# Attention units that take two key groups at once, with scores in both row halves and PSUM copies on ScalarE

## The chip, the cores and the metric

The kernel runs on one core of one Trainium2 chip. The metric is device microseconds for one execution, a median over several runs; a profiled execution gives the trace that is read here. The engines are named as in the profile: PE (TensorE matmul) and PEld (its weight loads), DVE (VectorE), ACT (ScalarE), POOL (GpSimd) and SP (SyncE, which issues most loads).

## What is computed

Two decoder layers over 256 tokens of width 2048, all in float32. Cut to what matters:

```python
for l in range(DEPTH):
    h = rms_norm(x, norm1_g[l])
    z = h @ w_in[l]                  # sgu u | sgu v | q (16 heads) | k (4) | v (4)
    out_a = chunked_sgu(gelu(z_sgu), ...)
    out_b = swa_sink_attention(q, k, v, ...)
    x = x + concat(rms_norm(out_a), rms_norm(out_b)) @ w_out[l]
    h2 = rms_norm(x, norm2_g[l])
    x = x + (silu(h2 @ w_gate[l]) * (h2 @ w_up[l])) @ w_down[l]
```

The attention is banded: queries in blocks of 128, window 128, so block 0 sees 128 keys and block 1 sees 256. Sixteen query heads share four key groups (head h uses group h // 4), head width 64. q and k are RMS-normed per head; the scores get a relative-position bias from a table of 32 buckets, a mask, and a sink logit in the softmax.

## The kernel before

**Projections.** Every big product is split for precision: `split2` (lines 91 to 102) makes of each loaded 128x1024 weight tile `raw` a rounded part `wh` on ACT (line 97) and the rest `wl` on DVE (line 98); `mm3` (136 to 138) adds three matmuls of 128x512. `unit` (140) is one weight tile: 12 such matmuls over two token blocks, then `tick()`. A column block of `w_in` (`in_block`) is eight units. The order of blocks is k and v (block 6), q heads 0 to 7 (4), q heads 8 to 15 (5), gate v (2, 3), gate u (0, 1). Then come `w_out` (64 units over both layers), and the feed-forward part with a seven-product scheme (`seven`) interleaved with ordinary units. In this last part `debt` decides which stream goes next, from the constants VEC, MM and LOAD and the calls of `vec` and `pe`.

**What sets the order of small work.** `later(delay, fn)` puts a function into the program when the count of units has grown by `delay`; the framework then orders the instructions of each engine by its own scheduler, so a piece may stand a little earlier or later than written. All waits come from the framework.

**PSUM.** Pool `pa` (tag acc, 5 banks) holds the accumulators of the projections, `pd` (dacc, 2 banks) and `pm` (sm, 1 bank) serve small results in attention: `small_ps` (131) takes pm, pd, pd in turn.

**Attention.** `kv_norm` and `q_norm` evacuate an accumulator on ACT, square it on DVE (217), reduce (219), take the power on POOL (184), scale on DVE, transpose on PE (201) and copy the transposed tile out of PSUM on DVE with the gain (300, 323). k is written twice, so that each of the four groups stands in both row halves (partitions 0 to 63 and 64 to 127) of `kT`. `attend(g, t, par)` (341) handles one group and one query block. For t=0 a unit has all four heads of the group, two in each row half. For t=1 it has two heads only, of one row half (`par` is (0,) or (1,)), over 256 keys; the scores of one row half share a PSUM bank `ps_s`. The rest of a unit: add bias (361), maximum (366), small rows (369, 371), one exponential per head on ACT (374), es and rden (378 to 381); three units later `turn` transposes the probabilities (388) and copies them out on DVE (389); five units later `weigh` multiplies with v (395) and scales (405). There are 12 such units per layer, one every 2.25 units of weights. `attend_end` squares and transposes the result.

**The bias** is made on the chip: `rel_table` (243) multiplies the table with one-hot rows (`ps_r`, 251), writes it to DRAM (255), spreads it there by a skewed read (259), and `load_bias` (336) reads a group at a time.

**The end.** The last product's columns are added to `xres` (700) and sent out (703), 128x512 at a time.

Of the kernel before, what the change touches and what calls it, by code (L numbers as in the profile page):

```python
# [19 lines left out]
DRAM = bass.MemoryType.DRAM  # L20
# [30 lines left out]
RL = 512  # L51
WARM = 12

# [12 lines left out]
def trunk(ctx, tc, x, xt, w_in, w_out, w_gate, w_up, w_down, sgu_w, sgu_g, consts,  # L66
          rel_bias, onehot, radd, out):
# [8 lines left out]
    dp = ctx.enter_context(tc.tile_pool(name="dp", bufs=1, space=DRAM))  # L76
# [133 lines left out]
    def finish_rms(ss, width):  # L210
        tot = small([P, 1], "tot")
        nc.vector.tensor_reduce(tot, ss, AX.X, ALU.add)
        return inv_rms(tot, 1, width)

    def head_inv(z, n):
        sq = zp.tile([P, NB], F32, tag="z", name="sq")
        nc.vector.tensor_tensor(sq[:, : n * HD], z, z, ALU.mult)
        ss = small([P, n], f"hs{n}")
        nc.vector.tensor_reduce(
            ss, sq[:, : n * HD].rearrange("p (h d) -> p h d", d=HD), AX.X, ALU.add  # L220
        )
        return inv_rms(ss, n, HD)
# [5 lines left out]
    rdram = dp.tile([NH, P, SEQ], F32, tag="rdram", name="rdram")  # L228
    pairs1 = []
    ss1 = [small([P, ND], "ss4") for t in range(NTOK)]  # L230
# [6 lines left out]
    def load_x(t, h, ss=ss1):  # L237
        c = slice(h * D // 2, (h + 1) * D // 2)
        nc.sync.dma_start(xres[:, t, c], x[t * P : (t + 1) * P, c])
        for n in range(2 * h, 2 * h + 2):  # L240
            sum_sq(ss[t][:, n : n + 1], xres[:, t, n * NB : (n + 1) * NB])

    def rel_table():
        relb = cp.tile([NBUCKET, NH], F32, tag="relb", name="relb")
        nc.gpsimd.dma_start(relb, rel_bias)
        oneh = zp.tile([NBUCKET, RL], F32, tag="z", name="oneh")
        nc.gpsimd.dma_start(oneh, onehot)
        rad = zp.tile([NH, RL], F32, tag="z", name="rad")
        nc.gpsimd.dma_start(rad, radd)
        ps_r = small_ps([NH, RL], "ps_r")  # L250
        nc.tensor.matmul(ps_r, relb, oneh, start=True, stop=True)
        rsb = zp.tile([NH, RL], F32, tag="z", name="rsb")
        nc.vector.tensor_tensor(rsb, ps_r, rad, ALU.add)
        rline = dp.tile([NH, RL], F32, tag="rline", name="rline")
        nc.sync.dma_start(rline, rsb)
        skew = bass.AP(
            tensor=rline.tensor, offset=rline.offset + P - 1, ap=[[RL, NH], [-1, P], [1, SEQ]]
        )
        nc.sync.dma_start(rdram, skew)
# [7 lines left out]
    later(11, rel_table)  # L267

    for lay in range(L):
# [5 lines left out]
        def begin(lay=lay, layer=layer, ss1=ss1):  # L275
            layer["rstd1"] = [finish_rms(ss1[t], D) for t in range(NTOK)]
# [5 lines left out]
        kT = ap.tile([P, NKV, SEQ], F32, tag="big", name="kT", bufs=8)  # L282

        def kv_norm(acc, lay=lay, layer=layer, zkv=zkv, kT=kT):
            kd = []
            zz = ap.tile([P, NTOK, NB], F32, tag="big", name="zkv", bufs=8)
            for t in range(NTOK):
                z = zz[:, t]
                nc.scalar.activation(z, acc[t], AF.Copy, scale=layer["rstd1"][t])
                zkv.append(z)  # L290
                inv = head_inv(z[:, : NKV * HD], NKV)
                k2 = zp.tile([P, NKV, 2, HD], F32, tag="z", name="k2")
                kin = z[:, : NKV * HD].rearrange("p (h d) -> p h d", d=HD)
                for r in range(2):
                    nc.vector.tensor_tensor(k2[:, :, r, :], kin, bc(inv, HD), ALU.mult)
                kd.append(k2.rearrange("p h r d -> p (h r d)"))

            def to_T(c):
                ps = transpose_pair([kd[t][:, 2 * c * P : (2 * c + 2) * P] for t in range(NTOK)])
                nc.vector.tensor_scalar(  # L300
                    kT[:, 2 * c : 2 * c + 2, :], ps, cst[:, lay, C_KG : C_KG + 1], None, ALU.mult
                )

            for c in range(2):
                later(5 + c, lambda c=c: to_T(c))
# [5 lines left out]
        def q_norm(b, acc, lay=lay, layer=layer, qT=qT):  # L311
            qn = []
            for t in range(NTOK):
                z = zp.tile([P, NB], F32, tag="z", name="zq")
                nc.scalar.activation(z, acc[t], AF.Copy, scale=layer["rstd1"][t])
                inv = head_inv(z, 8)
                z3 = z.rearrange("p (h d) -> p h d", d=HD)
                nc.vector.tensor_tensor(z3, z3, bc(inv, HD), ALU.mult)
                qn.append(z)

            def to_T(c):
                ps = transpose_pair([qn[t][:, 2 * c * P : (2 * c + 2) * P] for t in range(NTOK)])
                nc.vector.tensor_scalar(
                    qT[b][:, 2 * c : 2 * c + 2, :], ps, cst[:, lay, C_QG : C_QG + 1], None,
                    ALU.mult,
                )

            for c in range(2):
                later(5 + c, lambda c=c: to_T(c))

        ssb = [small([P, NKV], "ss4") for t in range(NTOK)]
# [4 lines left out]
        def load_bias(g, bias=bias):  # L336
            bt = ap.tile([P, GRP, SEQ], F32, tag="big", name="bias", bufs=8)
            nc.gpsimd.dma_start(bt, rdram[g * GRP : (g + 1) * GRP].rearrange("h q k -> q h k"))
            bias[g] = bt

        def attend(g, t, par, zkv=zkv, kT=kT, qT=qT, ob=ob, bias=bias, layer=layer):
            nk = (t + 1) * P
            k0 = SEQ - nk
            nh = 2 * len(par)
            heads = [h for h in range(GRP) if h % 2 in par]
            step = heads[1] - heads[0]
            nkb = nk // P
            nsink = layer["nsink"]
            s = ap.tile([P, nh, nk], F32, tag="spt", name="s", bufs=4)
            for r in par:  # L350
                ps = small_ps([P, 2, nk], "ps_s")
                for i in range(2):
                    h = g * GRP + 2 * i + r
                    nc.tensor.matmul(
                        ps[:, i, :],
                        qT[h // 8][HD * r : HD * r + HD, (h % 8) // 2, t * P : (t + 1) * P],
                        kT[HD * r : HD * r + HD, g, :nk],
                        start=True,
                        stop=True,
                    )  # L360
                nc.vector.scalar_tensor_tensor(
                    s[:, par.index(r) :: len(par), :], ps, 1.0 / math.sqrt(HD),
                    bias[g][:, r::2, k0:], ALU.mult, ALU.add,
                )
            m = small([P, GRP], "m")[:, :nh]
            nc.vector.tensor_reduce(m, s, AX.X, ALU.max)
            hs = slice(g * GRP + heads[0], (g + 1) * GRP, step)
            nm = small([P, GRP], "nm")[:, :nh]
            nc.vector.scalar_tensor_tensor(nm, m, -1.0, nsink[:, hs], ALU.mult, ALU.min)
            es = small([P, GRP], "es")[:, :nh]  # L370
            nc.vector.tensor_tensor(es, nm, nsink[:, hs], ALU.subtract)
            den = small([P, GRP], "den")[:, :nh]
            for i in range(nh):
                nc.scalar.activation(
                    s[:, i, :], s[:, i, :], AF.Exp, bias=nm[:, i : i + 1],
                    accum_out=den[:, i : i + 1],
                )
            nc.scalar.activation(es, es, AF.Exp)
            rden = small([P, GRP], "rden")[:, :nh]
            nc.vector.tensor_tensor(rden, den, es, ALU.add)  # L380
            nc.vector.reciprocal(rden, rden)
            pt = ap.tile([P, nh * nkb, P], F32, tag="spt", name="pt", bufs=4)

            def turn():
                pst = small_ps([P, nh * nkb, P], "ps_p")
                s4 = s.rearrange("p h (b k) -> p (h b) k", k=P)
                for i in range(nh * nkb):
                    nc.tensor.transpose(pst[:, i, :], s4[:, i, :], ident)
                nc.vector.tensor_copy(pt, pst)

            def weigh():
                pv = small_ps([P, nh, HD], "ps_v")
                for i in range(nh):
                    for b in range(nkb):
                        nc.tensor.matmul(
                            pv[:, i, :],
                            pt[:, i * nkb + b, :],
                            zkv[b][:, (NKV + g) * HD : (NKV + g + 1) * HD],
                            start=b == 0,
                            stop=b == nkb - 1,  # L400
                        )
                if (g, t) not in ob:
                    ob[g, t] = zp.tile([P, GRP * HD], F32, tag="z", name="ob")
                o3 = ob[g, t].rearrange("p (h d) -> p h d", d=HD)
                nc.vector.tensor_tensor(o3[:, heads[0] :: step, :], pv, bc(rden, HD), ALU.mult)

            later(3, turn)
            later(5, weigh)

        def attend_end(g, lay=lay, ob=ob, ssb=ssb, pairs_b=pairs_b):  # L410
            for t in range(NTOK):
                sum_sq(ssb[t][:, g : g + 1], ob[g, t])
# [398 lines left out]
```

## Time and profile before

| | us |
|---|---|
| median of 3 runs | 1977.56 (1976.96 to 1980.13) |
| the profiled execution (its span) | 1981.0 |
| PE busy | 1956.6 |
| DVE busy | 1723.4 |
| ACT busy | 1151.8 |
| POOL busy | 127.0 |

The profiled execution is 3.4 us longer than the median of the runs. Weight tiles go through the chip in the order described: layer 1's `w_in` stage from 7 to 204 us, `w_out` to 295, feed-forward to 992, then the same again for layer 2, whose `w_in` stage ends at 1188 and `w_out` at 1279. The granted clock of PE is full throughout. In timeline rows the columns are start, duration (both us), engine, line, operation, tiles, shapes and count; what stands in brackets is idle time of the engine before the row and what ended it. [...]

### The profile page before, as it was taken

Reading aid. Unit: us, or ns where it says so; the run is one execution under the profiler, and the core shown is the slowest. Engines: PE = TensorE matmul, PEld = TensorE weight load, DVE = VectorE, ACT = ScalarE, POOL = GpSimd, SP = SyncE. Lnnn points to the kernel's source line nnn. Section 1 sums busy time; section 2 is a strip of 40 time slices with the busy share of each in tenths; the row PEclk is TensorE's granted clock in tenths of the full one; section 3 lists DMA queues with packets and bytes.
Section 4 is the critical chain, followed back from the end, with each engine's and each line's share of the span. In section 5 each row is a group of like instructions: output and inputs, shape, how many; then the busy total and the mean of one; then the engine's idle time right before and its main releaser. Section 6 shows DMA issues by size and latency. Waiting matters only on the chain.

```text
span 1981.0 us, 25159 instructions
## 1 busy us (share of the span) xinstructions
PE 1956.6 (99%) x8894; PEld 1592.8 (80%) x8894; DVE 1723.4 (87%) x1977; ACT 1151.8 (58%) x1463; POOL 127.0 (6%) x137
## 2 busy tenths in 40 slices
PE   9999999999999999999999999999999999999999
PEld 6788888778887888888888788877788878788887
DVE  6777689999999999999767766899999999999996
ACT  6465566665565565665654655665656555656553
POOL 1211001000000000000002100000000000000000
PEclk9999999999999999999999999999999999999999
DMA  8753657668777768768656445586687776687684
GB/s 316 255 167 129 190 167 225 218 209 247 223 231 235 223 213 259 220 220 265 202 190 190 141 152 178 177 253 195 214 251 218 231 246 202 207 272 209 221 268 141
DMA packets 119712, 424.46 MB, mean 214 GB/s; under 512 B 13169, under 2 KB 15345, under 8 KB 119585
## 3 DMA queue, kind: packets, MB, share of 16 engines
q1 hardware_dynamic: 107072, 377.65, 55.0%
q0 software_dynamic: 12512, 45.19, 12.9%
q8 instruction: 70, 1.15, 0.3%
q14 instruction: 58, 0.47, 0.1%
HBM read 420.66 MB, written 4.23 MB: 214 GB/s over the span
## 4 chain that ended last, share of the span: by engine, by line
PE 82%; DVE 8%; DMA 4%; issue 3%; ACT 2%; POOL 1%; ACTq 0%; SPq 0%; DVEq 0%; POOLq 0%
PE acc L136 9%; PE acc L138 9%; PE acc L137 9%; PE dacc L136 8%; PE dacc L137 8%; PE dacc L138 8%; PE m L137 6%; PE m L138 6%; PE m L136 6%; DVE wl L98 4%; PE n L137 3%; PE n L136 3%; PE n L138 3%; DMA raw<-in_w_down_dram 3%; ACT wh L97 2%
## 5 line engine op out<-in xcount | busy, mean ns | idle before, releaser
L97 ACT CAST wh<-raw 128x1024 fp32r<-128x1024 f32 (+1 forms) x778 | 801.0, 1049 | 652.7 <-DVE raw L609 232.8
L98 DVE TENSOR_TENSOR wl<-raw,wh 128x1024 fp32r<-128x1024 f32 (+1 forms) x778 | 927.4, 1217 | 130.1 <-PE acc L137 54.9
L136 PE MATMUL dacc<-wh,aT 128*128 128x512 f32 x608 | 237.1, 392 | 0.6 <-ACT wh L97 0.2
L137 PE MATMUL dacc<-wl,aT 128*128 128x512 f32 x608 | 237.2, 390 | 0.0
L138 PE MATMUL dacc<-wh,aT 128*128 128x512 f32 x608 | 236.8, 390 | 0.0
L137 PE MATMUL m<-wl,ext 128*128 128x512 f32 x576 | 227.6, 395 | 5.1 <-DVE wl L98 5.1
L136 PE MATMUL m<-wh,ext 128*128 128x512 f32 x576 | 226.9, 394 | 4.7 <-ACT wh L97 4.7
L138 PE MATMUL m<-wh,ext 128*128 128x512 f32 x576 | 224.5, 390 | 0.0
L98 DVE TENSOR_TENSOR wl<-t,wh 128x1024 fp32r<-128x1024 f32 x144 | 175.5, 1219 | 16.8 <-issue 8.0
L136 PE MATMUL acc<-wh,hT 128*128 128x512 f32 x448 | 180.3, 404 | 0.7 <-ACT wh L97 0.7
L97 ACT CAST wh<-t 128x1024 fp32r<-128x1024 f32 x144 | 151.4, 1051 | 47.9 <-PE dacc L138 30.7
L137 PE MATMUL acc<-wl,hT 128*128 128x512 f32 x448 | 175.6, 392 | 0.6 <-DVE wl L98 0.6
L138 PE MATMUL acc<-wh,hT 128*128 128x512 f32 x448 | 175.5, 392 | 0.0
L617 POOL DMA_DIRECT2D t<-in_w_gate_dram x72 | 61.4, 852 | 1374.5 <-DVE wl L98 721.0
L136 PE MATMUL acc<-wh,aT 128*128 128x512 f32 x352 | 139.2, 395 | 0.0
L138 PE MATMUL acc<-wh,aT 128*128 128x512 f32 x352 | 137.4, 390 | 0.0
L137 PE MATMUL acc<-wl,aT 128*128 128x512 f32 x352 | 137.2, 390 | 0.0
L136 PEld LDWEIGHTS dacc<-wh,aT 128*128 128x128 f32 x608 | 114.1, 188 | 26.4 <-DVE xres L700 2.3
L137 PEld LDWEIGHTS m<-wl,ext 128*128 128x128 f32 x576 | 108.1, 188 | 32.9 <-DVE wl L98 11.6
L137 PEld LDWEIGHTS dacc<-wl,aT 128*128 128x128 f32 x608 | 114.2, 188 | 24.7 <-DVE wl L98 1.5
L138 PEld LDWEIGHTS dacc<-wh,aT 128*128 128x128 f32 x608 | 114.1, 188 | 23.6
L136 PEld LDWEIGHTS m<-wh,ext 128*128 128x128 f32 x576 | 108.2, 188 | 30.1 <-ACT wh L97 8.0
(150 smaller groups left out, 3040.7 us busy)
## 6 DMA issues: line engine op xcount, KB each, us to landing
raw<-in_w_gate_dram SPq DMA_DIRECT2D x176, 512.0 KB, 5.6
raw<-in_w_up_dram SPq DMA_DIRECT2D x176, 512.0 KB, 4.5
raw<-in_w_down_dram SPq DMA_DIRECT2D x176, 512.0 KB, 5.3
raw<-in_w_in_dram SPq DMA_DIRECT2D x108, 512.0 KB, 4.3
t<-in_w_gate_dram POOLq DMA_DIRECT2D x72, 512.0 KB, 6.4
raw<-in_w_out_dram SPq DMA_DIRECT2D x64, 512.0 KB, 3.7
bias<-rdram POOLq DMA_DIRECT2D x8, 512.0 KB, 4.4
xr<-in_xt_dram SPq DMA_DIRECT2D x8, 256.0 KB, 5.7
```

Of the source, the lines that this page charges most:

```text
L97: nc.scalar.copy(wh[:, j : j + step, :], src)
L98: nc.vector.tensor_tensor(wl[:, j : j + step, :], src, f(wh[:, j : j + step, :]), ALU.subtract)
L136: nc.tensor.matmul(acc, ah, wh, start=first, stop=False)
L137: nc.tensor.matmul(acc, ah, wl, start=False, stop=False)
L138: nc.tensor.matmul(acc, al, wh, start=False, stop=last)
L617: nc.gpsimd.dma_start(t2, w_gate[lay, b, i, 1], accum_op=ALU.add)
```

## The change

- The host lays out the q columns of `w_in` so that the first q block holds groups 0 and 1, the second 2 and 3, and head i of group 2gp stands in row half 0 beside head i of group 2gp+1 in row half 1. k is then written once: `kT` holds two groups per transposed tile, in the two row halves.
- `attend(gp, t, i0, n)` takes two groups. t=0: four heads of each group, eight in all; t=1: two heads of each. There are 6 units per layer, at the counts in `UNIT_AT`. Scores alternate between the two row halves and go to two banks.
- `turn` comes two units after (before: three), in two banks of four transposes, and `weigh` four after (before: five).
- Copies out of PSUM of k, q and the probabilities go to ACT, as do the squares in `head_inv`; reductions and powers of the two token blocks share tiles.
- `small_ps` has a fourth bank in its turn, from `pa`.
- The bias comes from the host as `band`, one contiguous load per group; `rel_table` goes. The scratch for DMA descriptors is halved.
- The last column block is added and sent out in halves.

```diff
-        pool, tag = ((pm, "sm"), (pd, "dacc"), (pd, "dacc"))[next(turns) % 3]
+        pool, tag = ((pm, "sm"), (pd, "dacc"), (pd, "dacc"), (pa, "acc"))[next(turns) % 4]
...
+UNIT_AT = (6, 9, 12, 15, 19, 23)
...
+            nc.scalar.activation(sq[:, : n * HD], z, AF.Square)
...
-    later(11, rel_table)
...
-                for r in range(2):
-                    nc.vector.tensor_tensor(k2[:, :, r, :], kin, bc(inv, HD), ALU.mult)
+                nc.vector.tensor_tensor(k, kin, bc(inv[t], HD), ALU.mult)
...
+                ps = transpose_pair(kd)
+                nc.scalar.activation(kT, ps, AF.Copy, scale=cst[:, lay, C_KG : C_KG + 1])
...
-                nc.vector.tensor_scalar(
-                    qT[b][:, 2 * c : 2 * c + 2, :], ps, cst[:, lay, C_QG : C_QG + 1], None,
-                    ALU.mult,
+                nc.scalar.activation(
+                    qT[b][:, 2 * c : 2 * c + 2, :], ps, AF.Copy,
+                    scale=cst[:, lay, C_QG : C_QG + 1],
                 )
...
+            nc.gpsimd.dma_start(bt, band[g])
...
+            s = ap.tile([P, 2, n, nk], F32, tag="spt", name="s", bufs=4)
+            ps = [small_ps([P, n, nk], f"ps_s{r}") for r in range(2)]
+            for i in range(n):
+                for r in range(2):
+                    rows = slice(HD * r, HD * r + HD)
                     nc.tensor.matmul(
+                        ps[r][:, i, :], qT[gp][rows, i0 + i, t * P : (t + 1) * P], kT[rows, gp, :nk],
+                        start=True, stop=True,
                     )
+            for r in range(2):
                 nc.vector.scalar_tensor_tensor(
+                    s[:, r], ps[r], 1.0 / math.sqrt(HD), bias[2 * gp + r][:, isl, SEQ - nk :],
+                    ALU.mult, ALU.add,
                 )
...
             def turn():
+                for half in range(2):
+                    pst = small_ps([P, 4, P], "ps_p")
+                    for i in range(4):
+                        nc.tensor.transpose(pst[:, i, :], s8[:, 4 * half + i, :], ident)
+                    nc.scalar.copy(pt[:, 4 * half : 4 * half + 4], pst)
...
-            later(3, turn)
-            later(5, weigh)
+            later(2, turn)
+            later(4, weigh)
...
+        units = [(gp, t, i0, n) for gp in range(2) for t, i0, n in ((0, 0, GRP), (1, 0, 2), (1, 2, 2))]
...
+                    parts = 2 if final and lay == L - 1 and n == ND - 1 else 1
...
-    nc = bacc.Bacc("TRN2", target_bir_lowering=False, num_devices=1)
+    nc = bacc.Bacc("TRN2", target_bir_lowering=False, num_devices=1, dynamic_dma_scratch_size=8192)
```

Where the instructions stand now. The first place is on PE, in layer 1, at scores of t=1. `acc` is the running projection, `ps_s` scores, `ps_v` the product with v, `ps_p` transposed probabilities, `ps_t` other transposes. Before, one row half at a time:

```order
L138 MATMUL acc_810<-wh,hT 128x512
L354 MATMUL ps_s<-kT,qT_129 128x256 x2
L395 MATMUL ps_v<-zkv,pt 128x64 x4
L388 MATMUL ps_p<-ident,s 128x128 x4
L136 MATMUL acc_809<-wh,hT 128x512
```

and in the change (its lines are those of the new program, where 330 is the scores, 134 to 136 are `mm3`):

```order
L136 MATMUL acc_765<-wh,hT 128x512
L330 MATMUL ps_s_887<-kT,qT_125 128x256
L330 MATMUL ps_s_888<-kT,qT_125 128x256
L330 MATMUL ps_s_887<-kT,qT_125 128x256
L330 MATMUL ps_s_888<-kT,qT_125 128x256
L199 MATMUL ps_t<-ident,zq 128x128 x4
L134 MATMUL acc_764<-wh,hT 128x512
```

Two matmuls of one row half have become four that alternate between the halves and their banks; a layer has four such pieces where it had eight. Only the last unit of layer 2 is torn: its first bank is filled here, in the change, and its second 34 projection matmuls later:

```order
L415 MATMUL ps_g<-v,wm 128x128 x4
L330 MATMUL ps_s_9435<-kT,qT_8293 128x256 x2
L135 MATMUL acc_9215<-wl,hT 128x512
L136 MATMUL acc_9215<-wh,hT 128x512
L135 MATMUL acc_9216<-wl,hT 128x512
```

The piece stays two of one half, as before. The second place is PE at scores of t=0 before, with tile numbers (924 is the bank of row half 0, 928 that of row half 1):

```order
L138 MATMUL acc1_810<-wh_907,hT_188 128x512
L354 MATMUL ps_s_924<-kT_128,qT0_129 128x128 x2
L354 MATMUL ps_s_928<-kT_128,qT0_129 128x128 x2
L136 MATMUL acc0_809<-wh_950,hT_214 128x512
L137 MATMUL acc0_809<-wl_951,hT_214 128x512
```

These four, two of one half and then two of the other, become eight that alternate. The third place is ACT in the first softmax of layer 1. Before:

```order
L97 COPY wh<-raw 128x1024 x8
L374 ACTIVATE s,den<-s,nm 128x128 x4
L378 ACTIVATE es<-es 128x4
L97 COPY wh<-raw 128x1024
L315 ACTIVATE zq<-acc_573,ir_460 128x512
```

and in the change:

```order
L302 ACTIVATE qT_125<-ps_t,cst 128x512
L95 COPY wh<-raw 128x1024
L349 ACTIVATE s,den<-s,nm 128x128 x8
L353 ACTIVATE es<-es 128x8
L293 ACTIVATE zq<-acc_538,ir_441 128x512
L364 COPY pt<-ps_p 128x512 x2
L293 ACTIVATE zq<-acc_539,ir_441 128x512
L218 ACTIVATE sq<-zq 128x512 x2
```

Eight exponentials, both copies of the probabilities and two squares now stand between one `wh` cast and the next. From the first matmul of the seven-product scheme to the next layer's first k transpose, and again in layer 2 from its last `ob` transpose to the end, PE's rows are the same in both programs.

More of the change, by code (lines that the diff above doesn't have):

```diff
@@ L19 @@
 PSUM = bass.MemoryType.PSUM
-DRAM = bass.MemoryType.DRAM
 P = 128
@@ L227, in trunk @@
     xres = cp.tile([P, NTOK, D], F32, tag="xres", name="xres")
-    rdram = dp.tile([NH, P, SEQ], F32, tag="rdram", name="rdram")
     pairs1 = []
-    ss1 = [small([P, ND], "ss4") for t in range(NTOK)]
+    ss1 = small([P, NTOK, ND], "ss4")
     def first_pair(p, pairs=pairs1):
@@ L240, in load_x @@
         for n in range(2 * h, 2 * h + 2):
[L241 to L259, printed above, removed]
+            sum_sq(ss[:, t, n : n + 1], xres[:, t, n * NB : (n + 1) * NB])
     for p in range(2):
@@ L275, in begin @@
         def begin(lay=lay, layer=layer, ss1=ss1):
-            layer["rstd1"] = [finish_rms(ss1[t], D) for t in range(NTOK)]
+            layer["rstd1"] = finish_rms(ss1, D)
             nsink = small([P, NH], "nsink")
@@ L337, in load_bias, with attend @@
             bt = ap.tile([P, GRP, SEQ], F32, tag="big", name="bias", bufs=8)
-            nc.gpsimd.dma_start(bt, rdram[g * GRP : (g + 1) * GRP].rearrange("h q k -> q h k"))
+            nc.gpsimd.dma_start(bt, band[g])
             bias[g] = bt
-        def attend(g, t, par, zkv=zkv, kT=kT, qT=qT, ob=ob, bias=bias, layer=layer):
+        def attend(gp, t, i0, n, zkv=zkv, kT=kT, qT=qT, ob=ob, bias=bias, layer=layer):
             nk = (t + 1) * P
[L343 to L359, printed above, removed]
@@ L366, in attend @@
+            m, nm, es, den, rden = (row(v) for v in ("m", "nm", "es", "den", "rden"))
             nc.vector.tensor_reduce(m, s, AX.X, ALU.max)
[L367 to L372, printed above, removed]
@@ L391, in weigh @@
-            def weigh():
[L392 to L405, printed above, removed]
@@ new lines, in weigh @@
+            def weigh():
+                pv = small_ps([P, 2, n, HD], "ps_v")
+                for r in range(2):
+                    cols = slice((NKV + 2 * gp + r) * HD, (NKV + 2 * gp + r + 1) * HD)
+                    for i in range(n):
+                        for b in range(t + 1):
+                            nc.tensor.matmul(
+                                pv[:, r, i], pt[:, (r * n + i) * (t + 1) + b, :], zkv[b][:, cols],
+                                start=b == 0, stop=b == t,
+                            )
+                if (gp, t) not in ob:
+                    ob[gp, t] = zp.tile([P, NB], F32, tag="z", name="ob")
+                o4 = ob[gp, t].rearrange("p (r i d) -> p r i d", r=2, d=HD)[:, :, isl]
+                nc.vector.tensor_tensor(
+                    o4, pv, rden.unsqueeze(3).to_broadcast([P, 2, n, HD]), ALU.mult
+                )
@@ L452, in v_gate @@
                 later(6 + half, lambda half=half: spatial(half))
-        ssa = [small([P, 2], "ss2") for t in range(NTOK)]
+        ssa = small([P, NTOK, 2], "ssa")
         pairs_a = []
```

176 lines of the change are left out of this document (91 added, 85 removed).

## The prediction

> **What bounds the kernel now.** I read the page first, then busy time by stage, then PE's own waits.
>
> ```profile
> span 1981.0 us, 25159 instructions
> PE 1956.6 (99%) x8894; PEld 1592.8 (80%) x8894; DVE 1723.4 (87%) x1977; ACT 1151.8 (58%) x1463; POOL 127.0 (6%) x137
> PE 82%; DVE 8%; DMA 4%; issue 3%; ACT 2%; POOL 1%; ACTq 0%; SPq 0%; DVEq 0%; POOLq 0%
> ```
>
> PE is busy 99% of the span, and 82% of the chain that ended last is PE. The stages say the same where the change lies:
>
> ```profile
> 60.00:200.00 140.00, 138.57 (x720) 111.79 (x719) 105.89 (x200) 77.53 (x161) 19.04 (x18) 1.00 0.54 177
> 320.00:985.00 665.00, 658.16 (x2920) 537.97 (x2919) 625.80 (x606) 397.81 (x424) 28.93 (x34) 1.00 0.74 230
> 1050.00:1180.00 130.00, 128.54 (x677) 104.27 (x676) 98.24 (x191) 71.67 (x154) 18.98 (x16) 1.00 0.51 160
> 1300.00:1976.00 676.00, 668.28 (x2954) 544.70 (x2953) 628.79 (x609) 394.12 (x414) 29.67 (x35) 1.00 0.72 225
> ```
>
> The columns are the stretch, its length, busy time of PE, PEld, DVE, ACT and POOL, clock, DMA share and GB/s. In the two attention stretches (rows one and three) PE is idle 1.43 and 1.46 us, while DVE is busy 76% and ACT 55%. So time goes there only if PE's own stream gets shorter; DVE work that is removed or moved to ACT buys nothing by itself. In the feed-forward stretches DVE is at 94% and PE idles 6.8 and 7.7 us, but there the change alters no instruction of PE and its order is the same, so I leave them as they are. Most of PE's idle time in attention is three waits of the probability transposes, here by stretch:
>
> ```profile
> PE ps_p L388 <- DVE s L361: 0.6, 1, 0.6
> PE ps_p L388 <- DVE nm L369: 0.9, 1, 0.9
> PE ps_p L388 <- DVE s L361: 0.5, 1, 0.5
> ```
>
> **The change part by part.** What a small piece costs PE is the distance between the projection matmuls around it, less what these take themselves. First the scores of t=1:
>
> ```profile
> 79.52 0.39 PE L137 MATMUL acc<-wl,hT 128*128 128x512 f32 x1
> 79.75 0.39 PE L138 MATMUL acc<-wh,hT 128*128 128x512 f32 x1
> 80.07 1.13 PE L354 MATMUL ps_s<-kT,qT 64*128 64x256 f32 x4
> 81.13 0.50 PE L136 MATMUL acc<-wh,hT 128*128 128x512 f32 x1
> 81.46 0.40 PE L137 MATMUL acc<-wl,hT 128*128 128x512 f32 x1
> ```
>
> Projection matmuls start 0.23 us apart. From 79.75 to 81.46 there are 1.71 us with two of them, so the piece costs 1.71 - 0.45 = 1.26 us for two matmuls of one row half (each is two records). Whether the other half can run beside it is shown by t=0, whose four matmuls are two of one half and then two of the other:
>
> ```profile
> 95.01 0.39 PE L138 MATMUL acc<-wh,hT 128*128 128x512 f32 x1
> 95.33 0.72 PE L354 MATMUL ps_s<-kT,qT 64*128 64x128 f32 x8
> 95.98 0.50 PE L136 MATMUL acc<-wh,hT 128*128 128x512 f32 x1
> 96.32 0.39 PE L137 MATMUL acc<-wl,hT 128*128 128x512 f32 x1
> 95.33 0.39 PE L354 MATMUL ps_s<-kT,qT 64*128 64x128 f32 x2
> 80.39 0.38 PE L354 MATMUL ps_s<-kT,qT 64*128 64x256 f32 x1
> 80.60 0.59 PE L354 MATMUL ps_s<-kT,qT 64*128 64x256 f32 x2
> ```
>
> The last three rows are what was under way in windows of 50 ns. At 95.33 two records run at once, and both are over after 0.39 us, about as long as one takes; in the t=1 piece the window shows one alone from 80.39, and the next starts 0.21 later. So the halves run side by side. A piece of four alternating matmuls over 256 keys should cost what two of one half cost, 1.26, plus a few hundredths: I take 1.27. Bounds: 1.26 below, and above 1.26 + 4 x 0.21 = 2.10 if 256 columns did not overlap. I take the low end, since the row of t=0 is the same kind of matmul. Before there are 8 such pieces per layer, 16 x 1.26 = 20.2 us. After there are 8 in all, but the last of layer 2 is torn into two of one half: 7 x 1.27 + 2 x 1.26 = 11.4. **Saved 8.8.**
>
> Scores of t=0: from 95.01 to 96.32 are 1.31, less 0.45, so 0.86 for a piece of four. The step within one half at 128 columns is half of 0.21; four more records in each half make 0.86 + 4 x 0.11 = 1.30 for eight (at most 0.86 + 0.65, were the whole block repeated). After: 4 x 1.30 = 5.2. Before: 7 x 0.86 = 6.0, and the first piece of layer 1, which stands in three parts among other work:
>
> ```profile
> 62.38 1.04 PE L201 MATMUL ps_t<-ident,zq 128*128 128x128 f32 x8
> 64.05 0.48 PE L354 MATMUL ps_s<-kT,qT 64*128 64x128 f32 x2 [0.63 <-DVE qT L323]
> 66.18 0.40 PE L138 MATMUL acc<-wh,hT 128*128 128x512 f32 x1
> 73.67 0.39 PE L138 MATMUL acc<-wh,hT 128*128 128x512 f32 x1
> 74.74 0.39 PE L137 MATMUL acc<-wl,hT 128*128 128x512 f32 x1
> ```
>
> From 62.38 to 66.18 are 3.80; less eight transposes at 0.11 and three projection matmuls that is 2.24. The third part takes 74.74 - 73.67 - 0.45 = 0.62. Together 2.9, with the wait of 0.63 for the copy of q in it. In the new order this piece stands whole, with 12 projection matmuls (2.7 us) between the last q transposes and it, against the 0.6 us of a copy on ACT (row below). **Saved 6.0 + 2.9 - 5.2 = 3.7.**
>
> Transposes and the table:
>
> ```profile
> 83.75 0.39 PE L138 MATMUL acc<-wh,hT 128*128 128x512 f32 x1
> 83.98 0.60 PE L388 MATMUL ps_p<-ident,s 128*128 128x128 f32 x4
> 84.65 0.40 PE L137 MATMUL acc<-wl,hT 128*128 128x512 f32 x1
> 38.28 0.39 PE L138 MATMUL acc<-wh,hT 128*128 128x512 f32 x1
> 38.60 1.03 PE L251 MATMUL ps_r<-oneh,relb 32*16 32x512 f32 x2
> 39.90 0.40 PE L137 MATMUL acc<-wl,hT 128*128 128x512 f32 x1
> ```
>
> Four transposes cost 0.90 - 0.45 = 0.45; k needs four fewer per layer, **0.9**. The table matmul costs 1.62 - 0.45 = 1.17, **1.2**. The probability transposes (48 per layer) and the products with v keep their number, and since four full-height ones cost hardly more than their own steps, larger or smaller pieces of them gain nothing.
>
> The three waits of the turn (2.0 us in the rows above) depend on how far ahead of the turn the scores stand, against the softmax chain:
>
> ```profile
> 76.44 0.40 ACT L374 ACTIVATE s<-s,nm 128x128 f32<-128x128 f32 x1 [1.29 <-DVE nm L369]
> 76.84 0.39 ACT L374 ACTIVATE s<-s,nm 128x128 f32<-128x128 f32 x1
> 77.29 1.23 DVE L98 TENSOR_TENSOR wl<-raw,wh 128x1024 fp32r<-128x1024 f32 x1 [0.69 <-PE acc L137]
> 81.23 0.69 DVE L361 SCALAR_TENSOR_TENSOR s<-ps_s,bias 128x512 f32<-128x512 f32 x1
> 82.44 0.68 DVE L366 TENSOR_REDUCE m<-s 128x2 f32<-128x512 f32 x1
> L626 ACT COPY m<-m 128x512 f32<-128x512 f32 x18 | 10.4, 576 | 1.5 <-PE m L138 1.4
> L446 ACT ACT_TABLE_LOAD x4 | 5.1, 1283 | 3.8 <-PE acc L138 3.8
> ```
>
> A unit of t=0 now needs two bias adds (1.4), a maximum over twice the row (about 1.3), 0.2 for the small row and eight exponentials 0.40 apart (3.2): 6.1 us to the last, 4.5 to the fourth. In the first unit 24 projection matmuls stand between, 5.5 us, and the second bank's transposes come 0.45 later, at 6.0. It just fits; in units where the product with v stands between as well there are some 7 us. I take 0.5 of waits for all turns: **saved 1.5**. Against that I set **0.5** for new waits in the projections. On ACT 27 operations of about 0.58 per layer come on (twelve probability copies, five gains of k and q, ten squares): 15 us, so from 77.5 of 140 to about 93 of 132. In the order above some 7 us of such work stand between two `wh` casts (eight exponentials, two evacuations, two copies, two squares), and the three weight tiles that PE can still draw on cover 3 x 12 x 0.23 = 8.3.
>
> The rest costs nothing, for these reasons. The copies of k and q on ACT are hidden by the 12 projection matmuls that follow their transposes (2.7 us); without that cover each would cost PE its 0.6, five per layer. The moved squares and the shared powers lie in a chain of four weight units (11 us) from the projection's end to its transposes, where before there were five; the scheduler now puts these one unit earlier, and a late one would show as a wait for `zq`, of the size of the 0.63 above. The bias loads stand on POOL, ahead of the power of the second q block; with `kT` out of their buffers, the four groups, `zkv` and both `qT` are seven of eight, so the second pair need not wait, and POOL's power is not held up; if it were, a power late by one unit costs 2.7 per layer. [...] At the end two adds of half the width take about a tenth longer than one, and the last store is half as large: a few tenths either way, taken as 0.
>
> Sum: 8.8 + 3.7 + 0.9 + 1.2 + 1.5 - 0.5 = 15.6 us. The profiled span goes from 1981.0 to 1965.4; the runs lie 3.4 below their profile (1977.56 against 1981.0), so 1962.0.
>
> **The rivals.** *The softmax chain takes PE's place (slower).* Units are twice as large and ACT holds exponentials, copies and gelu in one queue. Place: the turn. Behind one `wl` (1.23), two table loads (1.28 each, to gelu and back) and a gelu of about 0.6 a chain grows by 4.4 us. The t=0 units (6.1 + 4.4 against 6.0) would wait 4.5 each; of the t=1 units (chain 4.9, with exponentials of 0.5, an estimate between once and twice the 0.40; 7.4 of cover) half would wait 1.9: 4 x 4.5 + 4 x 1.9 = 25.6, so 10 us slower net, 1988. It makes the kernel slower from 1.3 us of wait per unit on. For it: the three waits above are of this kind. Against: the new order puts at least 5.5 us between. [...]
>
> *Smaller gain by new waits.* A fourth bank of small tiles comes from the projections' five; where two of them are held when a block starts, its first matmuls wait for one evacuation, 0.6. Seven blocks per layer make 14 x 0.6 = 8.4 at most: 1962 to 1970, 1967 if over half of them wait.
>
> *256 columns do not overlap.* Then 7 pieces cost 0.84 more: 5.9, 1967.9. That is the case in which the change does not do what it says; the t=0 row speaks against it.
>
> *Feed-forward waits shrink too.* Its 14.5 us of idle PE could fall if it starts with more weights ready: 5 us, 1957. Same order, so unlikely.
>
> **How the numbers follow.** A measurement of this kernel tells 0.2% (4 us) from no change. Chances: forecast 0.64 (its own range 1958 to 1966), smaller gain 0.14, no overlap 0.05, feed-forward too 0.06, nothing visible 0.04, slower 0.07. All but the last two are faster by more than 4 us: 0.89; same 0.04; slower 0.07. The range of 8 in 10 runs from 1956 (the feed-forward case) to 1970 (both smaller-gain cases): it leaves out the slow rival and the rare ends.
>
> **What would show it.** In the profile of the change: score pieces of t=1 with eight records in about 1.15 us, seven such in place of eight torn ones; a projection matmul 1.7 us after the one before the piece; attention stretches shorter by about 8.5 us in layer 1 and 6.5 in layer 2; ACT near 70% there; PE's waits for probabilities under 1 us; feed-forward stretches of the same length. Wrong would be: score records one after the other, or PE waiting more than 1 us per unit for exponentials, or for a bank.

## The result, and the profile after

The kernel after takes 1971.88 us (median of 6 runs, 1970.31 to 1973.83) against 1977.26 us for the kernel before (6 runs, 1975.64 to 1980.13): ratio 0.9968, 95% interval 0.9958 to 0.9978. It is faster, by 5.4 us; 15.6 were forecast, and 1971.88 lies above the range.

The page of the profiled execution after: span and instructions, PE's row, engines of the chain that ended last.

```profile
span 1968.8 us, 24956 instructions
PE 1942.7 (99%) x8884; PEld 1586.9 (81%) x8884; DVE 1678.4 (85%) x1812; ACT 1175.8 (60%) x1489; POOL 115.5 (6%) x116
PE 85%; DVE 6%; issue 3%; ACT 2%; DMA 2%; POOL 1%; SPq 0%; DVEq 0%; ACTq 0%; POOLq 0%
```

The two profiles differ by 12.2 us, the runs by 5.4. A run of the kernel after takes 1.7 us more than its own span (1970.47 with 1968.8). By that the profiled execution before took about 1982.7, 5 us above the runs that were shown with it; a profile is one execution, and "the runs lie 3.4 below their profile" was no property of the kernel.

Busy time by stage (length; PE, PEld, DVE, ACT, POOL; clock; DMA share and GB/s), cut at the first and last projection matmul of a layer's input block and at the ends of the feed-forward. Before, then after:

```profile
7.40:204.10 196.70, 194.92 (x962) 156.65 (x963) 142.89 (x256) 111.78 (x215) 27.91 (x26) 1.00 0.64 216
295.30:991.90 696.60, 689.76 (x3066) 563.66 (x3064) 655.00 (x648) 418.62 (x457) 32.56 (x38) 1.00 0.73 228
991.90:1188.10 196.20, 194.74 (x978) 158.22 (x977) 139.07 (x250) 104.44 (x197) 28.42 (x24) 1.00 0.53 168
1279.30:1976.20 696.90, 689.18 (x3048) 561.82 (x3047) 648.57 (x639) 407.76 (x434) 32.73 (x38) 1.00 0.72 224
```

```profile
7.40:199.20 191.80, 187.31 (x956) 153.36 (x957) 120.72 (x176) 123.36 (x228) 24.30 (x17) 1.00 0.59 210
290.30:987.10 696.80, 689.99 (x3064) 563.46 (x3063) 654.42 (x646) 418.31 (x457) 31.54 (x37) 1.00 0.71 228
987.10:1179.40 192.30, 190.25 (x975) 155.52 (x974) 117.48 (x171) 116.46 (x210) 24.24 (x17) 1.00 0.50 172
1270.50:1964.00 693.50, 687.35 (x3049) 562.13 (x3047) 648.07 (x637) 408.16 (x434) 31.53 (x37) 1.00 0.71 225
```

Attention is shorter by 4.9 and 3.9 us, not by 8.5 and 6.5. In layer 1 PE's busy time fell by 7.6 us, but its idle time rose from 1.8 to 4.5. In layer 2 the busy time fell by 4.5 only: there much of the waiting stands between single transposes, and busy time covers it. The matmuls do what was forecast, in PE's order of time (start, duration):

```profile
71.02 1.16 PE L330 MATMUL ps_s<-kT,qT 64*128 64x128 f32 x16
72.11 0.50 PE L134 MATMUL acc<-wh,hT 128*128 128x512 f32 x1
81.40 1.13 PE L330 MATMUL ps_s<-kT,qT 64*128 64x256 f32 x8
```

A t=1 piece of eight records takes 1.13 us, a t=0 piece of sixteen 1.16: the halves overlap. The rest of the gain went into PE's waits (total, times, longest), first layer and then second:

```profile
PE ps_p L363 <- ACT s L349: 2.3, 1, 2.3
PE ps_v L372 <- DVE aT L190: 0.9, 1, 0.9
...
PE ps_v L372 <- DVE aT L190: 0.9, 1, 0.9
PE ps_p L363 <- ACT s L349: 0.9, 1, 0.9
```

The first one is followed back through the engines' rows in order of time (idle time and its releaser in brackets):

```profile
82.53 3.91 POOL L182 TENSOR_TENSOR ir<-ms,mhalf 128x16 f32<-128x16 f32 x1 [21.39 <-DVE ms L180]
86.47 1.29 DVE L298 TENSOR_TENSOR zq<-zq,ir 128x512 f32<-128x512 f32 x2 [2.83 <-POOL ir L182]
87.68 1.28 DVE L335 SCALAR_TENSOR_TENSOR s<-ps_s,bias 128x512 f32<-128x512 f32 x2
90.01 1.21 DVE L344 TENSOR_REDUCE m<-s 128x4 f32<-128x1024 f32 x1
91.93 0.51 ACT L349 ACTIVATE s<-s,nm 128x256 f32<-128x256 f32 x1 [5.37 <-DVE nm L345]
92.58 0.44 PE L363 MATMUL ps_p<-ident,s 128*128 128x128 f32 x2 [2.33 <-ACT s L349]
```

The scores of the second unit are ready at 82.5. VectorE stands 2.83 us for the merged power of the second q block, and both bias adds are queued behind that multiplication. ScalarE, meant to be the risk, stands idle for 5.37 us. At 125 us the same happens with v, and a transposed pair is evacuated late, whose bank the product with v needs:

```profile
125.01 1.29 DVE L428 TENSOR_TENSOR v<-v,ir 128x512 f32<-128x512 f32 x2 [3.04 <-POOL ir L182]
129.41 0.86 DVE L190 SCALAR_TENSOR_TENSOR aT<-ps_t,cst,aT 128x256 fp32r<-128x256 f32 x2
130.02 1.97 PE L372 MATMUL ps_v<-zkv,pt 128*128 128x64 f32 x16 [0.86 <-DVE aT L190]
```

### The profile page after: what moved, and what is told of

Its sections match the earlier page's. It is cut to its first block, busy times and chain, and to the rows that moved or that the text cites. A ratio compares the mean times of both kernels' runs of the same rounds, so it can differ in the third digit from the quotient of the medians.

```text
span 1968.8 us, 24956 instructions
## 1 busy us (share of the span) xinstructions
PE 1942.7 (99%) x8884; PEld 1586.9 (81%) x8884; DVE 1678.4 (85%) x1812; ACT 1175.8 (60%) x1489; POOL 115.5 (6%) x116
## 3 DMA queue, kind: packets, MB, share of 16 engines
q8 instruction: 69, 1.13, 0.2%
## 4 chain that ended last, share of the span: by engine, by line
PE 85%; DVE 6%; issue 3%; ACT 2%; DMA 2%; POOL 1%; SPq 0%; DVEq 0%; ACTq 0%; POOLq 0%
PE dacc L134 9%; PE dacc L135 9%; PE dacc L136 9%; PE acc L135 8%; PE acc L136 8%; PE acc L134 8%; PE m L135 7%; PE m L136 7%; PE m L134 7%; PE n L135 3%; PE n L136 3%; PE n L134 3%; DVE wl L96 3%; ACT wh L95 1%; DVE raw L596 1%
```

## The experiments

Each ratio is to the kernel before on the same chip, which took 1981.8 to 1982.3 us on these chips (1977.3 in the runs above). The changed kernel itself ran on only one of these chips, so variants on the other are compared with it by ratio (0.9972).

**Both kernels again**, unedited (three profiles).

> The kernel before, unchanged, for a second profile. If the profiled execution of 1981.0 us was one of its slow ones (its runs have a median of 1977.26, and the kernel after lies 1.7 above its own span in every run), this profile's span should be near 1975.5 and the missing 5.5 us should stand in the feed-forward stretches (idle PE 6.8 and 7.7 us in the first profile), with both attention stretches the same to 0.3 us. If profiling itself adds 3.4 us to this kernel, as the prediction took it, the span is again 3 to 4 us above the median of its runs.

> The changed kernel, unchanged, for a second profile. If the waits in attention are fixed by the order, the wait of 2.3 us for the exponentials at 92.8 us and the two waits of 0.9 us of the products with v come again to 0.2 us. If they are accidents of transfers, they differ. The feed-forward stretches should differ by up to 3 us either way if they vary from execution to execution.

> The changed kernel unchanged, for a comparison on the same chip as the three others: 5.4 to 6.5 us under before, a wait of 2.3 us at 90 us, and half-speed windows of 3.41 us of the clock behind it in about two thirds of the executions (mean clock 0.999 on average).

Before: span 1981.5, median 1982.20, ratio to itself 1.0002 (0.9992 to 1.0011); attention 197.0 and 196.2. Here the profiled execution (1983.21 as a run) lies 1.0 above its median: the span of 1981.0 is what the kernel shows on such a chip, and the offset of 3.4 belongs to the pairing of that profile with those runs. After: medians 1975.97 and 1977.92, ratios 0.9972 (0.9961 to 0.9982) and 0.9973 (0.9962 to 0.9985); attention 191.8 and 192.2, waits of 2.3 and 0.9 us again. In the third profile it is 191.4 and 193.8, with the same waits, and the second of these stretches holds 3.4 us at half clock (told at the end; the mean clock of this run is 0.999). The waits are set by the order. The feed-forward stretches vary by up to 5 us between executions (693.5 and 698.6 us for the same one). With the other stretches of the profiles taken off the medians, both feed-forward stretches together took 1393.0 us before and 1396.2 after: 3.2 us more, though PE's order there is the same, and that of the other engines but for the merged rows of statistics at the start. Up to 1.3 of these 3.2 can be half clock elsewhere: by their mean clock the runs lose 2.1 us after and 0.9 before, and the profile that was taken off has none.

**Multiplications asked for later** (same for v, by 4).

```diff
-            for t in range(NTOK):
-                nc.vector.tensor_tensor(z3, z3, bc(inv[t], HD), ALU.mult)
+            later(3, scale)
```

> The changed kernel with the multiplications by the inverse norms of q and v asked for three and four weight units later, so that the bias adds of the second unit go to VectorE ahead of them. Theory A (VectorE stands 2.8 us waiting for the merged power on GpSimd, and the bias add behind it is late): the waits of the turn at 92.8 and 1072.9 fall from 2.0 and 2.0 us to under 0.7, 2.5 to 4 us less in all. Theory B (ScalarE is late with the exponentials because of the copies and squares that moved to it): no change, within 1 us.

1972.89 us, ratio 0.9948 (0.9934 to 0.9963). Layer 1 went from 191.8 to 189.3 us, layer 2 to 191.8. Eight transposes of a turn cost PE 0.8 us where nothing holds them; above that the turns cost 2.5 and 2.0 us in the changed kernel and 1.1 and 1.4 here. That is theory A's direction and not its size (under 0.7 each): in both layers a multiplication still stood ahead of the maximum.

**Turn and weighing later.**

```diff
-            later(2, turn)
-            later(4, weigh)
+            later(3, turn)
+            later(5, weigh)
```

> The changed kernel with the turn and the weighing one weight unit later (3 and 5, as before the change): 2.7 us more of projection matmuls between scores and turn. If the chain from scores to exponentials is too long by 2 us in two units, whatever makes it long, both waits of the turn vanish: 4 us less in attention. The waits of the products with v, which hang on a bank held by a transposed pair, should stay (2.2 us). If a later turn only moves the wait on (banks, buffers of probabilities), attention keeps its length within 1 us.

1972.42 us, ratio 0.995 (0.9937 to 0.9963). Layer 1 185.9 us, layer 2 193.6: there the wait moved to the bias add (1.3) and to a bank (1.8), with 3.4 us at half clock behind it (mean clock of the stretch 0.99). More distance alone cures the first layer and not the second.

**Powers split again** (`inv_rms(ss, n, HD)` for each t in place of one for both).

> The changed kernel with the merged powers of 128x16 undone: two of 128x8 for each block of q and v, as before the change; the squares stay on ScalarE. If it is the length of one merged power (3.9 us in the first layer, against 1.7 for one of 128x8) that holds VectorE, the wait of VectorE for the first multiplication falls by about 2 us, the one for the second stays near 1, and the turn's waits (2.0 and 2.0 us) fall by 1 to 2 us in all. If only the place of the multiplications ahead of the bias adds counts, the sum of the two waits stays and so does the time, within 0.7 us.

1977.29 us, ratio 0.9984 (0.9973 to 0.9995); attention 191.7 and 191.9. VectorE's waits for q's power fell from 5.6 to 2.6 us in layer 1, the turn's waits did not (1.5 and 1.4 us against 2.3 and 0.9; above what their pieces cost, 2.6 and 1.7 against 2.5 and 2.0). What counts is the place of the multiplication ahead of the bias adds and the maximum, not the merging. The time says little here: the feed-forward of this profile is 3.2 us longer than that of the second profile after.

**Multiplications held behind the maximum.**

```diff
+            ahead[0] = nc.vector.tensor_reduce(m, s, AX.X, ALU.max)
...
+        with tc.issue_after(ahead[0].ins):
+            nc.vector.tensor_tensor(z3, z3, bc(inv[t], HD), ALU.mult)
```

> The changed kernel with the multiplications of the second q block and of v held, on VectorE, behind the maximum of the newest unit (late_scale asked for it, but the multiplications still stood ahead of the maximum). Turn and weighing stay at 2 and 4. If the wait for the merged power is what made the exponentials of the second unit late, the turn's waits at 92.8 and 1072.9 go to under 0.3 us and attention gets 4 us shorter than in the changed kernel (191.8 and 192.2 us); if the transposed pairs' evacuation was late for the same reason, the two waits of 1.1 us of the products with v go as well, 6 us in all, unless the later v makes the spatial products wait instead. If ScalarE's longer queue is the cause, attention stays within 1.5 us of late_scale (189.3 and 191.8).

> The same with the turn and the weighing at 3 and 5. The two remedies act on the same waits, so little should come on top of the better of them: attention near 185.5 us in each layer, and a time some 3 us under the changed kernel's variant with the later turn if its two waits in the second layer (1.3 for the bias add, 1.8 for a bank) vanish.

Held: 1974.25 us, ratio 0.9959 (0.9947 to 0.9971), attention 189.6 and 190.4. In layer 1 the multiplications (`zq`) now stand behind the maximum and wait for nothing, and the transposes of the turn run without a pause:

```profile
85.25 1.21 DVE L359 TENSOR_REDUCE m<-s 128x4 f32<-128x1024 f32 x1
87.31 0.68 DVE L308 TENSOR_TENSOR zq<-zq,ir 128x512 f32<-128x512 f32 x1
89.26 1.03 PE L378 MATMUL ps_p<-ident,s 128*128 128x128 f32 x8
```

The waits of the turn and of the products with v are gone from the list; what came is one row in each layer:

```profile
PE ps_g L430 <- DVE v L446: 2.0, 1, 2.0
...
PE ps_g L430 <- DVE v L446: 0.9, 1, 0.9
```

The v that was held is late for the spatial products. With the later turn as well no wait is left in attention: 186.7 and 187.6 us, 1964.56 us, ratio 0.9906 (0.989 to 0.9922). That they act on the same waits, so that little comes on top, was wrong: each remedy left waits that the other takes.

**Three banks for small tiles** (`(pa, "acc")` taken out of the turn).

> The changed kernel with small tiles in turn on three banks, as before the change (none from the projections' five). Theory of the late evacuation: the products with v at 131 us wait because VectorE evacuates the transposed pair late, whichever bank holds it; with fewer banks the waits stay or grow, and attention is 0 to 4 us longer. The rival of the prediction (the shared bank makes blocks wait for an evacuation): with three banks attention is shorter. If the places of the accumulators in the banks make the feed-forward 3 us slower, its stretches fall back to about 1393 us here.

1975.03 us, ratio 0.996 (0.9946 to 0.9975); attention 192.0 and 192.0, the first with 3.4 us at half clock. The fourth bank changes nothing in sum, but not because the theory held: the waits of the products with v are gone from the list in both layers, and more of the score pieces are torn. So which bank a product with v is given has a part in its wait, beside VectorE's lateness. The feed-forward of this profile takes 1396.1 us: the places of the accumulators do not make it slower.

**Score matmuls in the old order** (loops over `r` and `i` exchanged), a single run.

> The changed kernel with the score matmuls of a piece in the order of before: all of one row half, then all of the other. If the halves run side by side in whatever order they stand, a piece of t=1 still costs 1.27 us and one of t=0 1.29. If they overlap only where they alternate, the t=1 piece costs 1.27 + 4 x 0.21 = 2.1 and the t=0 piece about 1.7, and the attention stretches grow by some 4 us each.

```profile
69.79 1.71 PE L330 MATMUL ps_s<-kT,qT 64*128 64x128 f32 x16
```

The t=1 piece, two matmuls of each half, costs the same as alternated (1.16 us without the step behind it). The t=0 piece, four and four, takes 1.71 in place of 1.16. Attention is 192.8 and 193.4 us. Neither theory: with two in a row the halves still overlap fully, with four only in part. The alternation is worth 0.55 us a piece of t=0, 2.2 us in all.

**Descriptor scratch** (8192 in the kernel before; 16384 in the one after).

> The kernel before with the halved descriptor scratch (8192) and nothing else; all engines keep their order. In the runs so far the two feed-forward stretches together, worked out from the medians and the fixed length of the rest, take about 1393 us before and 1396.2 to 1396.7 in the changed kernel and its two variants: 3.3 us more with the same order of instructions. Theory S (the smaller scratch makes the accumulating loads of GpSimd slower): this kernel is 3 us slower than before. Theory P (place of the tensors in memory, or chance): the same as before within 1 us.

> The changed kernel with the default descriptor scratch (16384), made to fit by three buffers in place of four for the small rows of statistics; all engines keep their order. Theory S: 3 us faster than the changed kernel, in the feed-forward stretches alone. Theory P: the same within 1 us. Attention should keep its length (191.8 and 192.2 us) unless a third buffer of the small rows holds up a unit.

1982.63 us, ratio 1.0006 (0.9997 to 1.0016), and 1976.24 us, ratio 0.9979 (0.9969 to 0.999). The first interval just reaches 3 us, but the second kernel is no faster than the changed one. The scratch is not it.

**Scratch tensor in memory again** (2 MB, 512 KB of it written once).

> The changed kernel with a scratch tensor of 2 MB in device memory as before the change, of which 512 KB are written once at the start. If the place of the tensors in memory is what makes the feed-forward 3.3 us slower, this is 3 us faster than the changed kernel. If not (the clock's half steps, which take 2.1 and 2.7 us per run in the changed kernel's runs against 0.8 and 0.6 before, or chance), it is the same within 1 us.

1978.87 us, ratio 0.9985 (0.9973 to 0.9998): not faster, but slower than the changed kernel by some 2.6 us, where it was to be the same within 1. These runs have a mean clock of 0.9978, the changed kernel's 0.9989, which is worth up to 2.3 us. A scratch tensor does not bring the time back.

**Instruction fetches.** In the profiles after, an extra wait of the first feed-forward sits at one place, about 413 us into it, where `wh` waits for a load of `w_down`. The transfers of two microseconds around one fetch of 16 KB (queue 8, which moved 1.15 MB in 70 packets before) beside that load, before and then after (queue, packets, MB, share of 16 engines):

```profile
q1 hardware_dynamic: 100, 0.35, 50.7%
q0 software_dynamic: 12, 0.05, 29.6%
q8 instruction: 1, 0.02, 3.0%
```

```profile
q1 hardware_dynamic: 168, 0.63, 78.3%
q0 software_dynamic: 30, 0.06, 16.9%
q8 instruction: 1, 0.02, 3.0%
```

Such a packet takes 0.9 to 2.2 us. The 70 are one for every 254 of the 2 x 8894 weight loads and matmuls of TensorE, so they are taken for TensorE's stream. Up to the feed-forward that has 2814 records before and 2789 after, and the fetch falls at 399.6 to 401.6 us into the stretch before and at 403.9 to 409.7 in the variants after, amid denser loads.

```diff
+    for i in range(13):
+        nc.tensor.matmul(heat[:, :16], junk[:, :P], junk[:, :16], start=True, stop=True)
```

> The changed kernel with 13 more warm-up matmuls of 16 columns, 26 instructions on TensorE, about as many as its stream is shorter than before's ahead of the first feed-forward (2789 records against 2814). Theory F (the feed-forward is slower because the 16 KB fetches of TensorE's instructions, 1.0 to 1.4 us each on one DMA engine, now fall some 4 to 8 us later against it, beside a weight load with no slack): the fetch near 405 to 409 us after the stretch's start comes back to about 400 to 402, the wait of 1.4 to 1.9 us there (0.2 to 0.7 before) falls below 0.8, and the time is 1 to 3 us under the changed kernel's on the same chip. Rival (chance, or the clock alone): same waits, same time within 1 us.

> The version without the waits (multiplications held, turn and weighing one unit later), with the same 26 instructions. Theory F: the gap of 2.05 us that it has at 699 us goes, and the median falls by 1 to 2 us from 1964.6 against a before of 1982.3. Rival: the same within 1 us.

> The kernel before with 1 warm-up matmul in place of 12: 22 instructions fewer on TensorE, so its fetches fall against the feed-forward about where the changed kernel's do. [...] Theory F: the wait near 705 us grows from 0.1 to 0.5 us to over 1, and the first feed-forward (695.8 to 697.6 us before) takes 698 to 700. Rival: the feed-forward keeps its length.

With 26 instructions more the fetch is back at 402.5, with 22 fewer before's has gone to 405.7. The waits around it, first in the padded kernel (ScalarE's for the load), then in before with one warm-up matmul (PE's for `wl`, then ScalarE's):

```profile
ACT wh L95 <- DMA raw<-in_w_down_dram: 0.2, 1, 0.2
```

```profile
PE m L137 <- DVE wl L98: 1.5, 1, 1.5
ACT wh L97 <- DMA raw<-in_w_down_dram: 2.2, 2, 1.6
```

The padded kernel has no wait of PE there. (Before has 0.6 and 0.2 us of it in two profiles, after 0.7, 1.2 and 0.8 in three.) The padded kernel takes 1973.87 us, ratio 0.9959 (0.9946 to 0.9971), 4.0 us under the unpadded one on that chip by medians, 3.2 by means; 1 to 3 were expected. Before with one warm-up matmul takes 1986.43, ratio 1.0019 (1.0009 to 1.0029), 4.1 more than before, and not by its start: its layer 1 ends its projections at 204.25 us, before's at 204.1. From the medians the two feed-forward stretches take 1392.9 us in the padded kernel against 1397.0 without, and 1396.9 in before with one warm-up matmul against 1393.0. In this one profile of it the first stretch takes 697.5, though, where 698 to 700 were expected. The best version, held, later turn and padded, takes 1960.06 us, ratio 0.9893 (0.9878 to 0.9909): 4.5 us under the same without the 26 instructions, more than the 1 to 2 expected, and the gap at 699 us is gone. Its attention:

```profile
7.40:193.60 186.20, 185.78 (x956) 153.86 (x957) 120.99 (x176) 123.77 (x228) 24.39 (x17) 1.00 0.62 217
979.90:1167.50 187.60, 187.60 (x975) 155.38 (x974) 117.85 (x171) 116.15 (x210) 23.24 (x17) 1.00 0.53 176
```

The traces of all runs say the same without medians. In five profiles (before twice, before with the halved scratch, and the two padded ones) the fetch falls at 399.6 to 402.5 us into the first feed-forward, and both stretches together take 1392.2 us on the mean (1390.0 to 1393.9). In the twelve profiles of the changed kernel and its other variants it falls at 403.9 to 409.7 us, and they take 1396.1 (1390.3 to 1399.6). Before with one warm-up matmul takes 1394.5. Of the 3.9 us between the means, 2.8 arise in the first stretch, 1.5 of them between 400 and 420 us into it; for the other 2.4 no one place was found.

## Why the prediction was wrong

**The matmul terms were right.** Scores of t=1 (1.13 us and the step behind, 1.27 forecast), of t=0 (1.16 and 1.29 to 1.30), the transposes of k and the table matmul came as summed. With the waits removed, attention is 10.5 and 8.6 us shorter than before, 19.1 against the 15.6 of the sum. Of the 3.5 more, 1.0 are waits that the sum left in, and about 1.3 the last unit of layer 2, whose scores stand whole there; the rest was not traced.

**The step that failed is "saved 1.5" on the turn's waits, with "0.5 for new waits".** It set the chain's own instructions (4.9 us for a t=1 unit) against PE's cover (7.4). On VectorE the multiplications of the second q block and of v stood ahead of that chain or inside it, waiting 2.8 and 3.0 us for GpSimd in layer 1; the bias adds of the second unit, whose scores were ready at 82.5, started at 87.68, behind the multiplications of 86.47. The power was asked only whether it would be late for its own transposes ("a late one would show as a wait for `zq`"), never what is queued behind `zq` on VectorE. Waits of the turn above what their pieces cost anyway came to 2.5 and 2.0 us, where 0.5 was set; those of the products with v were 1.1 and 1.2, not foreseen. These 6.8 us stand against 1.0 in the sum, and attention fell short of the sum by 6.8. That the multiplications' place makes them is shown: with nothing but these held back, all four waits go, for one of the spatial products in each layer in their stead, and the held version with the later turn has no wait. For the products with v the choice of bank is a second condition.

**The slow rival had the right place and the wrong engine.** The softmax chain did end last at the turn, but by VectorE's wait, not by ScalarE's queue; copies out of PSUM, by VectorE, were late for the products with v alone (2.3 us). Of the rival with the fourth bank, the waits of the projection blocks did not come, but the turn of four banks has a part in the waits of the products with v. Missing overlap at 256 columns did not come.

**That the feed-forward stays as it is, since its order is the same, failed too.** PE's order is the same, but instruction fetches fall elsewhere. That the number of TensorE's instructions ahead of it makes 3 to 4 us is shown in both directions (4.0 and 4.5 less with 26 more, 4.1 more with 22 fewer). That the fetches are what does it is argued: one place was traced, it holds 1.5 of the 3.9 us, and that a packet holds up the load beside it is inferred from its length and its neighbours.

**The offset of 3.4** has no part in the gain. Together: 8.8 us less in attention, some 3.2 given back outside it, is 5.6; measured are 5.4, 6.4 and 4.4 on three occasions. The first profile after is no picture of this: its feed-forward is 3.2 us shorter than that of the profile before, where the medians have it longer.

## What to carry to other kernels

Sum a chain with what stands ahead of it on each engine (here multiplications that waited 2.8 and 3.0 us), and ask of every instruction that waits for another engine who is queued behind it. A later consumer and a better order are different remedies: against before, this change gained 17.7 us with both, 9.9 and 8.0 with one. A stretch whose order does not change can still change when instructions ahead of it come or go: here by 4.0 to 4.5 us for 22 and 26 of them.

## What had not been expected of the hardware

TensorE's granted clock was 0.50 for 3.4 us after a pause of 2.3 us:

```profile
85.00:92.00 7.00, 4.71 (x27) 3.76 (x27) 6.73 (x11) 1.66 (x6) 2.40 (x4) 1.00 0.48 157
92.20:95.60 3.40, 3.40 (x13) 2.75 (x12) 1.09 (x3) 2.70 (x8) 0.00 (x0) 0.50 0.94 223
95.60:100.00 4.40, 4.40 (x26) 3.22 (x25) 3.46 (x4) 1.73 (x2) 0.53 (x1) 1.00 0.50 181
```

These are stretches of the three-bank kernel around its wait for the exponentials: the clock column reads 0.50 in the middle row, and 13 matmuls run in 3.4 us where 26 run in the 4.4 after. Over 18 profiles there are 19 places where TensorE starts no matmul for 1.89 to 2.72 us; 11 of them are followed within 4.2 us by such a window, and of 37 pauses of 1.3 to 1.88 us one is. By the mean clocks of its runs the half speed costs at most 1.0 to 2.1 us per run of the kernel after, and 0.5 to 0.9 of before and of the two versions without the waits. That the pause causes the window is argued from these counts; no run changed a pause alone. In the first profile before, the clock reads 0.50 from 1980 us to the end, where PE has no matmul left, and costs nothing.

The fetches of 16 KB were not reckoned with either; that one holds up a load is argued. No row of PE's waits is without another engine as its cause, but ScalarE waited 2.2 us for loads of `w_down` around one in before with one warm-up matmul, and 0.2 us in the padded kernel.
